# Moving the strip buffers and temporaries of an encoder kernel by 192 bytes within each SBUF partition

## The chip, the cores and the metric

The kernel runs on one core of one Trainium2 chip. The metric is the device time of one execution in microseconds; lower is better. Before the change it is 2692.87 us, the median of three runs (2691.46 to 2693.15).

## The reference

Two layers of a bidirectional encoder on 256 tokens with 2048 features, all in float32, and a final norm:

```python
for l in range(DEPTH):                                  # 2
    u = rmsnorm(x, norm_mix[l])
    proj = u @ w_in[l]                                  # 2048 x 8256
    c_q, c_kv, k_pe, q_na, k_na, v_na, gate_a, gate_b = jnp.split(proj, IN_SPLITS, axis=-1)
    q  = rmsnorm(c_q, norm_qa[l]) @ w_uq[l]             # latent attention, 8 heads
    kv = rmsnorm(c_kv, norm_kva[l]) @ w_ukv[l]
    ...
    y_a = mla_attention(q_nope, rope(q_pe), k_nope, rope(k_pe), v) @ w_o_mla[l]
    y_b = neighbourhood_attention(q_na, k_na, v_na, rpb[l]) @ w_o_na[l]
    merged = sigmoid(gate_a) * y_a + sigmoid(gate_b) * y_b
    x = x + merged @ w_out[l]                           # 2048 x 2048
    h = rmsnorm(x, norm_mlp[l]) @ w_ff1[l]              # 2048 x 8192
    x = x + jnp.square(relu(h)) @ w_ff2[l]              # 8192 x 2048
return rmsnorm(x, norm_final)
```

## The kernel before

**Precision.** Every large product is made of float32r matmuls on operands that are split in two: `hi`, the value cast to float32r, and `lo`, what the cast left out. A product is hi x hi + hi x lo + lo x hi, three matmuls of TensorE that add up in one PSUM bank.

**The two homes of the operands.** Activations live in *slots*: 46 tiles of 128 partitions x 512 float32, 2048 bytes a partition each, in the pool `slots` (`pair()`, `wide()`, lines 88 and 92). Weights come from HBM as *strips*: 1 MB lands in `raw` by a DMA from SyncE's queue, ScalarE casts it into `hi`, VectorE subtracts into `lo` (lines 194 and 195 in the attention half of a layer, 170 and 171 in the MLP half and the output projection). Three `raw` buffers let the loads run ahead. Strips live in the pools `wpool` and `wpool2`, temporaries in `tmp` and `tmp2`; the first of each pair is opened for the attention half of a layer and closed after it, the second for the other half, at the same addresses.

**Who streams and who is loaded.** A matmul of TensorE first loads a 128 x 128 piece of one operand into the array (the stationary operand, PEld in the profile) and then streams the other through it (the moving operand). Three helpers use the two homes differently:
- `mm_b` (lines 216 and 217) loads a piece of a strip and streams a slot: 512 wide with `hi`, which covers hi and lo of the activation at once, then 256 wide with `lo`. It makes the projections whose result is wanted transposed.
- `mm_a` (lines 225 to 227) and `mm3` in `gemm_s` (line 381) load a piece of a slot and stream 512 columns of a strip, three matmuls per product. They make the gates, the output projections and, in `gemm_s` with Strassen's scheme on some of the blocks, the MLP. In the latent attention's values `mm_a` streams 256 columns.
- `mm_3` (lines 230 to 232) serves attention: for the scores both operands are slots, for softmax times values the moving one is `pp`, a temporary.

**Order of the work.** The order is written out in the kernel's Python code, with small generators for the attention heads and transposes that are advanced between groups of matmuls (`tick`), and a scheduler that places the instructions. Nothing in it reads an address.

**Where things lie in a partition.** Pools are laid out one behind the other as they are opened: `const`, `slots`, `keep`, then the pools of weights and temporaries. `const` ends, and so the slots begin, on a multiple of 256 bytes. Within a pool the tiles are laid out in the order of their first use, each rounded up to 32 bytes. `keep` holds, in this order, two `sums`, `junk`, two `var`, six `rcol`, four `diag` and four `rrow`: 64 + 2048 + 64 + 192 + 2048 + 4096 bytes. The buffers of strips are multiples of 4096 bytes, so all of them begin at the same place within 256 bytes as the pool itself. The buffers of `tmp` follow the strips in the same partition.

Of the kernel before, what the change touches and what calls it, by code (L numbers as in the profile page):

```python
# [33 lines left out]
F32 = mybir.dt.float32  # L34
# [5 lines left out]
P = 128  # L40
# [31 lines left out]
def trunk(ctx: ExitStack, tc: tile.TileContext, x, w_in, w_uq, w_ukv, rpb, w_o_mla, w_o_na,  # L72
# [4 lines left out]
    keep = ctx.enter_context(tc.tile_pool(name="keep", bufs=2))  # L77
# [17 lines left out]
    def small():  # L95
        return tmp.tile([P, S], F32, tag="small", name="small", bufs=smalls)

    ident = const.tile([P, P], F32, name="ident")
    make_identity(nc, ident)
    ones = const.tile([P, P], F32, name="ones")  # L100
# [788 lines left out]
```

## Time and profile before

| | before |
|---|---|
| median of three runs | 2692.87 us |
| the profiled execution, its own time | 2693.53 us |
| its span, first to last instruction | 2691.8 us |
| mean granted TensorE clock | 0.996 |
| matmuls | 12606 |
| TensorE busy | 2653.6 us |
| weight loads (beside the matmuls) | 2208.0 us |
| VectorE busy | 1912.8 us |
| ScalarE busy | 1387.9 us |
| moved by DMA | 508.92 MB, 189 GB/s on average |

In the profile's groups of instructions a line names the source line, the engine (PE is the matmul, PEld the load of weights, DVE is VectorE, ACT ScalarE), the operation, the tile written and the tiles read, the shapes, the count, then the sum of busy time in us and the mean of one in ns, and last the engine's idle time before them with what ended it. `pair`, `vh`, `vl` and `wide` are slots; `hi`, `lo`, `raw` and, in `gemm_s`, `sums` are strips. The chain of waits follows the work that ended last back from the last instruction; its pieces have a start, a length and what they were.

### The profile page before, as it was taken

What the parts mean: (1) busy time and instruction counts of PE and PEld (TensorE: products, weight loads), DVE (VectorE), ACT (ScalarE), POOL (GpSimd) and SP (SyncE); (2) the same over time, 40 slices, a digit from 0 to 9 for tenths busy, and PEclk for the clock granted to TensorE, in tenths of its full rate; (3) what the DMA queues carried; (4) which work ended last, traced back from release to release, by engine and by line L of the source; (5) the groups of instructions that cost most, each with busy time, mean ns of one, the idle gap of its engine ahead of it and who ended that gap; (6) DMA issues with size and microseconds to landing.
All of it is one profiled execution on the core that took longest, in us unless ns stands there. A gap on an engine that the chain in (4) does not pass through costs nothing.

```text
span 2691.8 us, 31697 instructions
## 1 busy us (share of the span) xinstructions
PE 2653.6 (99%) x12606; PEld 2208.0 (82%) x12606; DVE 1912.8 (71%) x2172; ACT 1387.9 (52%) x1611; POOL 95.1 (4%) x122
## 2 busy tenths in 40 slices
PE   8999999999999999999999999999999999999998
PEld 7888888878888888888878888888788888888886
DVE  5675486556788887887666754855567888878885
ACT  5554464445555545546445544644455555455453
POOL 1100000000000010000001000000000000100000
PEclk9999999999999999999999999999999999999999
DMA  7555544554667585675555555455645665766754
GB/s 231 184 155 189 192 153 156 187 187 166 205 193 234 166 240 190 201 234 174 187 173 175 169 188 184 145 164 170 210 168 196 203 219 180 234 203 196 250 167 146
DMA packets 199300, 508.92 MB, mean 189 GB/s; under 512 B 13456, under 2 KB 17552, under 8 KB 199152
## 3 DMA queue, kind: packets, MB, share of 16 engines
q1 hardware_dynamic: 189184, 488.14, 55.5%
q0 software_dynamic: 8960, 17.14, 3.2%
q8 instruction: 98, 1.61, 0.2%
q10 hardware_dynamic: 1008, 1.61, 0.2%
q14 instruction: 50, 0.41, 0.0%
HBM read 492.18 MB, written 2.10 MB: 184 GB/s over the span
## 4 chain that ended last, share of the span: by engine, by line
PE 90%; issue 7%; DVE 1%; ACT 1%; DMA 1%; POOL 0%; POOLq 0%; DVEq 0%; ACTq 0%
PE bank L381 42%; PE bank L227 11%; PE bank L225 11%; PE bank L226 11%; PE bank L216 8%; PE bank L217 4%; PE bank L344 1%; PE bank L230 1%; PE bank L232 1%; PE bank L231 1%; DMA raw<-in_w_in 1%; ACT hi L170 0%; PE bank L494 0%; PE bank L443 0%; DVE lo L195 0%
## 5 line engine op out<-in xcount | busy, mean ns | idle before, releaser
L381 PE MATMUL bank<-hi,pair 128*128 128x512 f32 x3692 | 1154.9, 392 | 3.2 <-ACT hi L170 3.2
L381 PEld LDWEIGHTS bank<-hi,pair 128*128 128x128 f32 x3692 | 692.2, 188 | 160.0 <-ACT hi L170 10.0
L171 DVE TENSOR_TENSOR lo<-raw,hi 128x2048 fp32r<-128x2048 f32 (+1 forms) x288 | 618.3, 2150 | 190.4 <-ACT hi L170 189.2
L170 ACT CAST hi<-raw 128x2048 fp32r<-128x2048 f32 (+1 forms) x288 | 517.3, 1801 | 452.5 <-PE bank L381 299.3
L381 PE MATMUL bank<-lo,pair 128*128 128x512 f32 x1846 | 723.3, 392 | 0.0
L195 DVE TENSOR_TENSOR lo<-raw,hi 128x1024 fp32r<-128x1024 f32 (+1 forms) x352 | 426.3, 1214 | 351.5 <-ACT hi L194 349.5
L194 ACT CAST hi<-raw 128x1024 fp32r<-128x1024 f32 (+1 forms) x352 | 364.3, 1041 | 410.4 <-PE bank L227 295.5
L225 PE MATMUL bank<-hi,pair 128*128 128x512 f32 (+1 forms) x1344 | 522.4, 390 | 0.0
L227 PE MATMUL bank<-hi,pair 128*128 128x512 f32 (+1 forms) x1344 | 520.9, 388 | 0.0
L226 PE MATMUL bank<-lo,pair 128*128 128x512 f32 (+1 forms) x1344 | 517.5, 385 | 2.4 <-DVE lo L171 2.4
L381 PEld LDWEIGHTS bank<-lo,pair 128*128 128x128 f32 x1846 | 346.8, 188 | 75.5 <-DVE lo L171 1.4
L216 PE MATMUL bank<-pair,hi 128*128 128x512 f32 x960 | 347.5, 403 | 5.5 <-ACT hi L194 4.8
L226 PEld LDWEIGHTS bank<-lo,pair 128*128 128x128 f32 x1344 | 252.9, 188 | 54.8 <-DVE lo L171 2.9
L227 PEld LDWEIGHTS bank<-hi,pair 128*128 128x128 f32 x1344 | 252.8, 188 | 54.4
L225 PEld LDWEIGHTS bank<-hi,pair 128*128 128x128 f32 x1344 | 252.9, 188 | 48.6
L217 PE MATMUL bank<-pair,lo 128*128 128x256 f32 x960 | 268.0, 283 | 0.0
L171 DVE TENSOR_TENSOR lo<-sums,hi 128x2048 fp32r<-128x2048 f32 x74 | 169.6, 2292 | 112.9 <-ACT hi L170 112.9
L170 ACT CAST hi<-sums 128x2048 fp32r<-128x2048 f32 x74 | 141.4, 1911 | 184.0 <-DVE sums L409 153.2
L216 PEld LDWEIGHTS bank<-pair,hi 128*128 128x128 f32 x960 | 181.8, 190 | 45.1 <-ACT hi L194 5.2
L217 PEld LDWEIGHTS bank<-pair,lo 128*128 128x128 f32 x960 | 181.5, 190 | 1.8
L424 DVE TENSOR_TENSOR wide<-wide,bank 128x512 f32<-128x512 f32 x240 | 154.0, 679 | 0.3
L405 DVE TENSOR_TENSOR sums<-raw 128x1024 f32<-128x1024 f32 x74 | 90.2, 1219 | 14.4 <-DMA raw<-in_w_ff 14.1
(122 smaller groups left out, 1463.0 us busy)
## 6 DMA issues: line engine op xcount, KB each, us to landing
raw<-in_w_ff SPq DMA_DIRECT2D x256, 1024.0 KB, 5.3
raw<-in_w_in SPq DMA_DIRECT2D x124, 1024.0 KB, 5.2
raw<-in_w_out SPq DMA_DIRECT2D x32, 1024.0 KB, 5.2
raw<-in_w_o_na SPq DMA_DIRECT2D x16, 1024.0 KB, 5.2
raw<-in_w_o_mla SPq DMA_DIRECT2D x16, 1024.0 KB, 5.2
xt<-wide POOLq DMA_DIRECT2D x48, 256.0 KB, 7.2
raw<-in_w_ukv SPq DMA_DIRECT2D x8, 1024.0 KB, 5.1
raw<-in_w_uq SPq DMA_DIRECT2D x8, 768.0 KB, 4.6
```

Source lines behind the costliest of these rows:

```text
L170: nc.scalar.copy(hi, src)
L171: nc.vector.tensor_tensor(lo, src, hi.bitcast(F32), op=ALU.subtract)
L194: nc.scalar.copy(hi, src)
L195: nc.vector.tensor_tensor(lo, src, hi.bitcast(F32), op=ALU.subtract)
L216: nc.tensor.matmul(ps, wh, a, start=first, stop=False)
L217: nc.tensor.matmul(ps[:, :S], wl, a[:, :S], start=False, stop=last)
L225: nc.tensor.matmul(ps, ah, wh, start=first, stop=False)
L226: nc.tensor.matmul(ps, ah, wl, start=False, stop=False)
L227: nc.tensor.matmul(ps, al, wh, start=False, stop=last)
L381: nc.tensor.matmul(b[i], x, y, start=count[i] == 1, stop=count[i] == total[i])
L405: nc.vector.tensor_tensor(ts[:, :1024].rearrange("p (a n) -> p a n", a=2), raw[:, :512].rearrange("p (a n) -> p a n", a=1).to_broadcast([P ...
L424: add = lambda o, a, c: nc.vector.tensor_tensor(o, a, c, op=ALU.add)
```

## The change

One tile of 48 float32, 192 bytes a partition, is taken from the pool `keep` before anything else is. It is never written or read. `keep` grows by 192 bytes, its other tiles and all pools opened behind it move up by as much, and strips begin at a multiple of 256 bytes, as slots do. `const` and the slots stay where they are. The instructions of all engines, their order and their waits are those of before; source lines behind the new ones count two higher.

```diff
     def small():
         return tmp.tile([P, S], F32, tag="small", name="small", bufs=smalls)
 
+
+    keep.tile([P, 48], F32, name="phase", bufs=1)
     ident = const.tile([P, P], F32, name="ident")
     make_identity(nc, ident)
     ones = const.tile([P, P], F32, name="ones")
```

## The prediction

> Places are given below as the remainder of an operand's address within a partition, divided by 256 bytes; "64/0" means that the moving operand (the one streamed through the array) begins at place 64 and the stationary one (the weights loaded into it) at place 0. About 0.2% (5.4 us) is what a measurement of this kernel can tell from no change.
>
> **What bounds the kernel now.** First the page: busy times, granted clock, chain of waits.
>
> ```profile
> span 2691.8 us, 31697 instructions
> PE 2653.6 (99%) x12606; PEld 2208.0 (82%) x12606; DVE 1912.8 (71%) x2172; ACT 1387.9 (52%) x1611; POOL 95.1 (4%) x122
> ...
> PEclk9999999999999999999999999999999999999999
> ...
> PE 90%; issue 7%; DVE 1%; ACT 1%; DMA 1%; POOL 0%; POOLq 0%; DVEq 0%; ACTq 0%
> ```
>
> TensorE is busy from end to end at full granted clock, and 97% of the chain is PE or its "issue" gaps. Everything else has slack, also in the densest stage, the MLP (table by stretches, first column PE, then PEld, DVE, ACT):
>
> ```profile
> 1110.00:1210.00 100.00, 100.00 (x437) 81.74 (x436) 83.01 (x65) 47.20 (x29) 7.07 (x8) 1.00 0.74 226
> ```
>
> There DVE has 17 us of 100 to spare and the DMA engines a quarter. So the time is 12,606 matmuls times the distance from one start to the next (the pitch), and only a changed pitch moves it. Next, which matmuls there are, from the groups by shape (x is the count, then total us and mean ns; a duration contains the pipeline, so it is longer than the pitch):
>
> ```profile
> L381 PE MATMUL bank<-hi,pair 128*128 128x512 f32 x3692 | 1154.9, 392 | 3.2 <-ACT hi L170 3.2
> L381 PE MATMUL bank<-lo,pair 128*128 128x512 f32 x1846 | 723.3, 392 | 0.0
> L225 PE MATMUL bank<-hi,pair 128*128 128x512 f32 x1280 | 504.5, 395 | 0.0
> L227 PE MATMUL bank<-hi,pair 128*128 128x512 f32 x1280 | 503.0, 393 | 0.0
> L226 PE MATMUL bank<-lo,pair 128*128 128x512 f32 x1280 | 499.6, 390 | 2.4 <-DVE lo L171 2.4
> ...
> L216 PE MATMUL bank<-pair,hi 128*128 128x512 f32 x960 | 347.5, 403 | 5.5 <-ACT hi L194 4.8 <-DVE pair L164 0.8
> ...
> L217 PE MATMUL bank<-pair,lo 128*128 128x256 f32 x960 | 268.0, 283 | 0.0
> ...
> L231 PE MATMUL bank<-pair 128*128 128x256 f32 x96 | 27.5, 286 | 0.0
> L232 PE MATMUL bank<-pair 128*128 128x256 f32 x96 | 27.2, 284 | 0.0
> L230 PE MATMUL bank<-pair 128*128 128x256 f32 x96 | 27.1, 282 | 0.0
> ...
> L225 PE MATMUL bank<-hi,pair 128*128 128x256 f32 x64 | 17.9, 280 | 0.0
> L226 PE MATMUL bank<-lo,pair 128*128 128x256 f32 x64 | 17.9, 280 | 0.0
> L227 PE MATMUL bank<-hi,pair 128*128 128x256 f32 x64 | 17.9, 280 | 0.0
> ...
> L232 PE MATMUL bank<-pp,vl 128*128 128x256 f32 x32 | 9.0, 281 | 0.0
> ...
> L231 PE MATMUL bank<-pp,vh 128*128 128x256 f32 x32 | 9.0, 280 | 0.0
> ```
>
> Four kinds, by where their operands lie now. Strips streamed against slots (L381, L225 to L227): 64/0. Slots streamed against strips (L216, L217, a 512-wide and a 256-wide one in turn): 0/64. Slots against slots (L230 to L232 with "pair" alone, the attention scores): 0/0. Softmax tiles against slots ("pp"): 192/0. The same 256-wide matmul stands here in all four: 283 at 0/64, 280 at 64/0, 280 to 281 at 192/0, and 282 to 286, mean 284, at 0/0, the arrangement that the change gives to the first two kinds.
>
> Durations have modelled ends, so I read pitches from the chain of waits in order of time (start us, us, what), as first and last row of an unbroken run:
>
> ```profile
> 700.98 42.83 PE bank L381 x187
> ```
> ```profile
> 53.50 0.12 PE bank L217
> ...
> 63.75 0.12 PE bank L217
> ```
> ```profile
> 371.99 0.12 PE bank L230
> ...
> 373.43 0.23 PE bank L216
> ```
> ```profile
> 374.84 0.12 PE bank L225
> ...
> 377.67 0.23 PE bank L216
> ```
> ```profile
> 383.78 0.12 PE bank L230
> ...
> 384.48 0.22 PE bank L464
> ```
>
> In order: 512 wide at 64/0, 42.83 / 187 = 229.0 ns. The pair at 0/64: 29 pairs in 10.25 us, 353.4 ns a pair. 256 wide at 0/0: 12 in 1.44 us, 120.0 ns. 256 wide at 64/0: 24 in 2.83 us, 117.9 ns. 256 wide at 192/0: 6 in 0.70 us, 116.7 ns (rounding leaves about 1 ns, 0.4 ns and 2 ns on the last three; the mean durations rank them the same way).
>
> **The change, part by part.** The pool `keep` holds 64 + 2048 + 64 + 192 + 2048 + 4096 = 8512 bytes a partition (small tiles take 32), which is 33 x 256 + 64, and it follows the slots, which lie on multiples of 256. That is why strips begin at 64. 192 more make them begin at 0; the addresses in the built program say the same, so the change does what it says. No instruction is added, removed or moved on any engine, no wait is added, and nothing writes the reserved bytes. What can change is how long instructions take.
>
> *Strips as moving operand, 64/0 to 0/0.* 5538 (L381) + 3840 (L225 to L227) = 9378 of 512 wide and 192 of 256 wide. No row shows a 512-wide one at 0/0, so it is bounded. The nearest rows are the two 256-wide runs: 120.0 - 117.9 = +2.1 ns at 0/0. Both kinds load 128 x 128 weights while the matmul before streams:
>
> ```profile
> L381 PEld LDWEIGHTS bank<-hi,pair 128*128 128x128 f32 x3692 | 692.2, 188 | 160.0 <-ACT hi L170 10.0
> ...
> L232 PEld LDWEIGHTS bank<-pair 128*128 128x128 f32 x96 | 18.2, 189 | 0.0
> ```
>
> That is one load per matmul and no longer for the wider one, so I take +2.1 ns per matmul whatever its width: 9570 x 2.1 = +20.1 us. If instead it goes with the streamed columns, 120.0 / 117.9 is +1.8%, +4.1 ns on 229.0: 9378 x 4.1 + 192 x 2.1 = +38.9 us. The other bound lies below nothing and is worked out under the faster rival. One row speaks on the 512-wide case directly, a slots-moving matmul (0) ahead of weights at 0 (TensorE in order of time):
>
> ```profile
> 102.74 0.39 PE L216 MATMUL bank<-pair,hi 128*128 128x512 f32 x1
> 102.97 0.28 PE L230 MATMUL bank<-pp,vh 128*128 128x256 f32 x1
> ```
>
> 0.23 us: between 229 and 231 cannot be told at this rounding, but it is not the 235 of its neighbours (353.4 - 118).
>
> *Strips as weights, 0/64 to 0/0.* 960 pairs at 353.4 ns. By the first value a pair becomes (229.0 + 2.1) + 120.0 = 351.1: 960 x -2.3 = -2.2 us. By the second it is 233.1 + 120.0 = 353.1: -0.3 us.
>
> *The rest.* `pp` goes from 192 to 128: 96 matmuls between 116.7 and 120.0, at most +0.3 us; the transposes of the softmax (128) and the small float32 matmuls shift by less than that each. DVE and ACT read and write strips at the new place too:
>
> ```profile
> L408 DVE TENSOR_TENSOR sums<-raw,sums 128x512 f32<-128x512 f32 x74 | 50.6, 684 | 0.5
> ...
> L800 DVE TENSOR_TENSOR xt<-xt,wide 128x512 f32<-128x512 f32 x8 | 5.1, 680 | 0.0
> ```
>
> The first has all three operands at 64, the second all at 0: 4 ns, on an engine with slack. Zero for the end. Weights land 5 us after their issue, three buffers ahead; only the load at the start, which nothing covers, could move, by tenths of a us.
>
> Sum against the profiled execution's own 2693.5 us: +20.1 - 2.2 = +17.9, 2711.4. The median of the runs is 0.7 below that execution, so the forecast is 2710.8, rounded to 2711. By the columns: +38.6, 2731.
>
> **A rule against the row.** The 0/0 run takes 120.0 ns and the 64/0 run 117.9. The Trainium skill, SBUF — State Buffer, section "SBUF: two separate sides", says that among the engines only the port pair shared by VectorE and GpSimd makes anyone wait, and that TensorE never does; by that the time would stay at 2693. The 2.1 ns speak against it as far as one kind of matmul can.
>
> **The rivals.**
>
> *Nothing changes (same).* The 2.1 ns at 0/0 could belong to the attention scores and not to the place: they come in short runs of 6 or 12 between other matmuls. For: the four kinds lie within 3% of each other at 256 wide. Against: the softmax-times-values matmuls run in the same helper, in runs as short, and are not slower than 64/0. Time: 2693, give or take 5.
>
> *The same place is the best place (faster).* The mechanism is that the cost falls with the distance between the two starts. For: at 0/64 (192 round the 256) a 512-wide matmul takes 353.4 - 118 = 235 ns against 229 at 64/0, so arrangement matters and 64 apart beats 192 apart; 0 could be better again. If the step to 0 is half of that step of 6.4, 3.2 ns: 9378 x -3.2 = -30.0 us, and the pairs fall to 225.8 + 117.9 = 343.7, 960 x -9.7 = -9.3 us; together -39, 2654. It decides as soon as the 512-wide pitch falls below 229.0 - 5.4 / 9378 x 1000 = 228.4 ns; a small gain of 1 ns gives 2681. Against: the only 0/0 run there is. DVE, with 17% spare in the MLP, would not take over for a gain of 1.5%.
>
> The pitch at 64/0 is 229.0 ns. The Trainium skill, TensorE: Matmul & The Clock Gate, "Part 2: What happens when you issue a matmul", gives about 216 ns from one 512-wide matmul to the next; if the place were all that keeps this kernel from it, the time would be 9378 x 13 = 122 us lower, 2571 (an estimate from that page). No run here shows 216.
>
> *By the columns (slower still).* 2731, as worked out above. For: the 512-wide durations differ more between kinds (392 to 403) than the 256-wide (280 to 286).
>
> **How the numbers follow.** Slower 0.52: per matmul 0.36, by the columns 0.16. Same 0.22. Faster 0.26, because 0/0 at 512 wide was never seen, and of the two kinds seen at 512 the one with strips as weights at 64 is the slow one. The likeliest case's own range is 2700 to 2732. For 8 in 10 I take that case nearly whole (0.50), same whole (0.22) and the small gains (0.11): from 2665 to 2732.
>
> **What would show it.** In the profile after, the order of instructions and the counts are those of before, and PE stays near 99%. Right: the long L381 runs of the chain at 231 ns instead of 229.0, with mean durations up from 392; the pair near 351; the 0/0 scores still at 120.0. By the columns: 233. Same: 229.0 and 353.4. The faster rival: below 228.4. Wrong altogether would be a change of time with an unchanged pitch, which would then lie in idle time of PE, now under 2%.

## The result and the profile after

The change makes the kernel faster: 2675.34 us (2673.55 to 2676.27, six runs) against 2692.16 us before (six runs), a ratio of 0.9936 with a 95% interval of 0.9924 to 0.9949. That is 16.8 us, where 18 us the other way had been forecast.

The page of the profiled execution after (2675.85 us; source lines count two higher than before):

```profile
span 2674.1 us, 31697 instructions
...
PE 2636.0 (99%) x12606; PEld 2206.9 (83%) x12606; DVE 1912.9 (72%) x2172; ACT 1388.7 (52%) x1611; POOL 95.4 (4%) x122
...
PEclk9999999999999999999999999999999999999999
...
PE 85%; issue 7%; DVE 5%; ACT 2%; DMA 1%; POOL 0%; POOLq 0%; DVEq 0%; ACTq 0%
```

The counts are the same, the clock is the same, VectorE and ScalarE are as busy as before to 0.1%. TensorE alone is busy for 17.6 us less, and the span is 17.7 us shorter: the whole effect is TensorE's. In the chain 5% of the span have passed from TensorE to the casts of DVE and ACT: strips are now ready only just in time at places. That costs little so far: the idle time before the Strassen matmuls (first row below) went from 3.2 to 4.3 us, and TensorE's idle time as a whole, span less busy time, stayed at 38 us.

The groups by shape after, in the order of those shown of before:

```profile
L383 PE MATMUL bank<-hi,pair 128*128 128x512 f32 x3692 | 1147.3, 390 | 4.3 <-ACT hi L172 3.3
L383 PE MATMUL bank<-lo,pair 128*128 128x512 f32 x1846 | 720.0, 390 | 0.0
...
L227 PE MATMUL bank<-hi,pair 128*128 128x512 f32 x1280 | 500.8, 392 | 0.0
L228 PE MATMUL bank<-lo,pair 128*128 128x512 f32 x1280 | 500.5, 391 | 2.4 <-DVE lo L173 2.4
L229 PE MATMUL bank<-hi,pair 128*128 128x512 f32 x1280 | 500.0, 391 | 0.0
...
L218 PE MATMUL bank<-pair,hi 128*128 128x512 f32 x960 | 346.3, 403 | 4.2 <-ACT hi L196 3.8 <-DVE pair L166 0.4
L219 PE MATMUL bank<-pair,lo 128*128 128x256 f32 x960 | 266.9, 282 | 0.0
...
L233 PE MATMUL bank<-pair 128*128 128x256 f32 x96 | 27.5, 286 | 0.0
...
L229 PE MATMUL bank<-hi,pair 128*128 128x256 f32 x64 | 18.1, 283 | 0.0
L228 PE MATMUL bank<-lo,pair 128*128 128x256 f32 x64 | 18.1, 283 | 0.0
```

The same lines of code move in opposite directions. 512 wide, L383 goes from 392 to 390, and L227 and L229 from 395 and 393 to 392 and 391. L228, the middle one of the three in `mm_a`, gains nothing at 512 wide: 390 before, 391 after. 256 wide, L228 and L229 go from 280 to 283. The pair that loads strips (L218, L219) and the attention scores (L233) stay within 1 ns.

The pitches from the chain after, each as an unbroken run or its first and last piece: the Strassen matmuls, the pair, the scores, the values.

```profile
696.15 42.43 PE bank L383 x187
```
```profile
53.13 0.12 PE bank L219
...
63.02 0.12 PE bank L219
```
```profile
369.23 0.12 PE bank L232
...
370.67 0.24 PE bank L218
```
```profile
372.09 0.12 PE bank L227
...
374.96 0.23 PE bank L218
```

42.43 / 187 = 226.9 ns, where it was 229.0. The pair: 28 in 9.89 us, 353.2 (353.4). The scores: 12 in 1.44 us, 120.0 (120.0). The values, 256 wide, now 0/0: 24 in 2.87 us, 119.6 (117.9). Worked out from these runs: 9378 x -2.1 = -19.7 us, 192 x +1.7 = +0.3, 960 x -0.2 = -0.2; together -19.6, beside -17.7 of the span. The same matmuls stand in the same order in both traces, so the distances from start to start can be added up by line over the whole of both. The Strassen matmuls come to -9.4 us, waits included; L227, L228 and L229 at 512 wide to -3.8, +0.8 and -2.6; the pairs to -1.7; the values to +0.3; all others to -1.4. Together that is the span's -17.7, up to rounding. So 2.1 ns for each of the 9378 is too much. The Strassen sum holds the 1.1 us of idle time named above, and the middle matmul of `mm_a` ran at 227.1 ns already before (mean from start to start, waits left out; 227.2 after), while the other two went from 230.4 and 229.6 to 227.1.

### The profile page after: what moved, and what is told of

It is laid out like the page before. It is cut to its first block, busy times and chain, and to the rows that moved or that the text cites. A ratio compares the mean times of both kernels' runs of the same rounds, so it can differ in the third digit from the quotient of the medians.

```text
span 2674.1 us, 31697 instructions
## 1 busy us (share of the span) xinstructions
PE 2636.0 (99%) x12606; PEld 2206.9 (83%) x12606; DVE 1912.9 (72%) x2172; ACT 1388.7 (52%) x1611; POOL 95.4 (4%) x122
## 4 chain that ended last, share of the span: by engine, by line
PE 85%; issue 7%; DVE 5%; ACT 2%; DMA 1%; POOL 0%; POOLq 0%; DVEq 0%; ACTq 0%
PE bank L383 36%; PE bank L228 11%; PE bank L229 11%; PE bank L227 11%; PE bank L218 8%; PE bank L219 4%; DVE lo L173 2%; ACT hi L172 2%; PE bank L346 1%; PE bank L232 1%; PE bank L234 1%; PE bank L233 1%; DVE pair L361 1%; PE bank L496 0%; DMA raw<-in_w_in 0%
## 5 line engine op out<-in xcount | busy, mean ns | idle before, releaser
L383 PE MATMUL bank<-hi,pair 128*128 128x512 f32 x3692 | 1147.3, 390 | 4.3 <-ACT hi L172 3.3
L383 PEld LDWEIGHTS bank<-hi,pair 128*128 128x128 f32 x3692 | 691.8, 188 | 153.7 <-ACT hi L172 11.0
L383 PE MATMUL bank<-lo,pair 128*128 128x512 f32 x1846 | 720.0, 390 | 0.0
L228 PE MATMUL bank<-lo,pair 128*128 128x512 f32 (+1 forms) x1344 | 518.5, 386 | 2.4 <-DVE lo L173 2.4
L227 PE MATMUL bank<-hi,pair 128*128 128x512 f32 (+1 forms) x1344 | 518.9, 387 | 0.0
L229 PE MATMUL bank<-hi,pair 128*128 128x512 f32 (+1 forms) x1344 | 518.1, 386 | 0.0
L383 PEld LDWEIGHTS bank<-lo,pair 128*128 128x128 f32 x1846 | 346.6, 188 | 72.8 <-DVE lo L173 1.8
L218 PE MATMUL bank<-pair,hi 128*128 128x512 f32 x960 | 346.3, 403 | 4.2 <-ACT hi L196 3.8
L228 PEld LDWEIGHTS bank<-lo,pair 128*128 128x128 f32 x1344 | 253.4, 189 | 51.5 <-DVE lo L173 2.9
L229 PEld LDWEIGHTS bank<-hi,pair 128*128 128x128 f32 x1344 | 253.4, 189 | 50.7
L227 PEld LDWEIGHTS bank<-hi,pair 128*128 128x128 f32 x1344 | 253.1, 188 | 49.1
L219 PE MATMUL bank<-pair,lo 128*128 128x256 f32 x960 | 266.9, 282 | 0.0
L218 PEld LDWEIGHTS bank<-pair,hi 128*128 128x128 f32 x960 | 181.2, 189 | 43.6 <-ACT hi L196 4.2
L219 PEld LDWEIGHTS bank<-pair,lo 128*128 128x128 f32 x960 | 181.9, 190 | 1.7
L407 DVE TENSOR_TENSOR sums<-raw 128x1024 f32<-128x1024 f32 x74 | 90.2, 1219 | 11.7 <-DMA raw<-in_w_ff 11.4
```

The costliest lines, as they stand in the source:

```text
L218: nc.tensor.matmul(ps, wh, a, start=first, stop=False)
L219: nc.tensor.matmul(ps[:, :S], wl, a[:, :S], start=False, stop=last)
L227: nc.tensor.matmul(ps, ah, wh, start=first, stop=False)
L228: nc.tensor.matmul(ps, ah, wl, start=False, stop=False)
L229: nc.tensor.matmul(ps, al, wh, start=False, stop=last)
L383: nc.tensor.matmul(b[i], x, y, start=count[i] == 1, stop=count[i] == total[i])
```

## The experiments

Three theories at the start. **A**: what counts is the distance between the starts of the streamed and the loaded operand within 256 bytes, and at 512 columns distance 0 is best. **B**: the streamed strip's own place counts, a multiple of 256 being best. **C**: the operands don't matter, the shifted temporaries do. In A, which operand is loaded when the matmul streams is left open. No kernel leaves work out. Pitches below are from the same run of 187 Strassen matmuls in the chain, unless said otherwise. In the code cuts, the remarks behind `#` are added here; they stand in no kernel.

### The distance: 128, 192, 32 and 224 bytes

The tile in `keep` takes another size.

```diff
-    keep.tile([P, 48], F32, name="phase", bufs=1)
+    keep.tile([P, 16], F32, name="phase", bufs=1)   # strips at 128; 32: 192; 56: 32; 40: 224
```

> Strips at place 128, slots at 0 (64 bytes reserved instead of 192). Theory A, the distance between the starts of the streamed and the loaded operand counts and 0 is best: the 512-wide strip matmul is at or above the 229.0 ns of 64 apart, the time 2692 us or more. Theory B, only the streamed strip's own place counts and a multiple of 256 is best: as with 64, 229 ns and 2692 us. Theory C, operands do not matter and the shift of the temporaries did it: between 2675 and 2693 us with the pitch of whatever the temporaries' place gives. The 256-wide matmul: A and B both have no number for it.

> Strips at place 192, slots at 0 (128 bytes reserved). Theory A: at or above 229.0 ns at 512 wide, 2692 us or more; if the distance counts round the 256 bytes, 192 is like 64 and gives 229.0 ns. Theory B: 229 ns, 2692 us. The 256-wide softmax matmuls that streamed from 192 before took 116.7 ns against 117.9 at 64, so 256 wide 116 to 118 ns here.

> 224 bytes reserved: strips at 32, slots at 0. If the pitch goes smoothly with the distance: halfway between 0 (227.1) and 64 (229.0), 228 ns, 2684 us. If there is a single best place and any distance costs the same or more: 229 ns or above, 2692 us or more. If the best place lies between 0 and 64: under 227 ns, under 2674 us.

> 160 bytes reserved: strips at 224, 32 bytes short of the slots' place. Smoothly between 192 (233.4 ns) and 0 (227.1): 230 ns, 2703 us. If any start behind the slots' place costs in full: 233 ns, 2730 us. If the best place lies here: under 227 ns, under 2674 us.

Measured: 2725.09 us at 128 (ratio to before 1.0120, 1.0105 to 1.0135), 2730.26 at 192 (1.0142, 1.0126 to 1.0159), 2728.21 at 32 (1.0133, 1.0118 to 1.0148), 2726.44 at 224 (1.0123, 1.0108 to 1.0138). The runs in the chain, in the order 128, 192, 32, 224:

```profile
706.77 43.62 PE bank L382 x187
```
```profile
706.88 43.63 PE bank L382 x187
```
```profile
708.58 43.63 PE bank L382 x187
```
```profile
707.42 43.62 PE bank L382 x187
```

All four are 233.3 ns. So of six distances, 0 gives 226.9, 64 gives 229.0 and the four others the same 233.3 in this run, though their times lie up to 5 us apart. B is out in the form put forward, since all places but 0 should have been alike and 64 is not. So is a cost that grows with the distance: 32 is dearer than 64. So is a best place between: nothing tried is under 226.9. The kernel before stood at the second best of the six places. At 256 columns the order is another one: the latent attention's values take, from start to start, 119.6 ns on average at distance 0, 118.7 at 128, 118.2 at 224, 117.9 at 64, 117.0 at 32 and 116.9 at 192 (180 starts each).

### Whose place: the slots moved, or both

```diff
     xt = [const.tile([P, D], F32, name=f"xt{t}") for t in range(2)]
+    const.tile([P, 48], F32, name="phase_slots")    # slots at 192, strips at 0
```

and, for both at 64, 16 float32 there and the 48 of the change in `keep`.

> 192 bytes are reserved ahead of the slots instead: slots at 192, strips at 0, which is 64 apart as before, but the strips lie where the change puts them. Theory A: pitch 229.0 ns at 512 wide and 2692 us, as before. Theory B: 226.7 ns and 2675 us, as after the change.

> Slots and strips both begin at 64 (64 bytes ahead of the slots, 192 more in the pool behind them). Theory A: starts are equal, so 226.7 ns at 512 wide and 2675 us, as after the change. Theory B: the strips are off the multiple of 256, so 229.0 ns and 2692 us.

Measured: 2691.89 us (0.9997, 0.9988 to 1.0006) with the slots at 192 and the strips at 0; 2674.19 us (0.9933, 0.9918 to 0.9947) with both at 64.

```profile
698.05 42.82 PE bank L382 x187
```
```profile
694.99 42.45 PE bank L383 x187
```

229.0 and 227.0 ns. The strips stand at 0 in the first and don't gain; they stand at 64 in the second, as before the change, and gain all of it. For the Strassen matmuls A is borne out and B excluded: it is the distance, wherever the two lie.

### Is it 256 bytes, and is it the temporaries

448 bytes in `keep` instead of 192; and 192 bytes at the head of `tmp` and `tmp2` alone.

```diff
-    keep.tile([P, 48], F32, name="phase", bufs=1)
+    keep.tile([P, 112], F32, name="phase", bufs=1)
```
```diff
         tmp = half_a.enter_context(tc.tile_pool(name="tmp", bufs=2, reuse_waits="tile"))
+        tmp.tile([P, 48], F32, name="phase", bufs=1)   # likewise in tmp2; nothing in keep
```

> 448 bytes are reserved, 256 more than in the change: strips at 0 within 256 bytes, 256 further within 512 or more. Theory A (the distance within 256 bytes decides): 227.1 ns at 512 wide and 2675 us, as after the change. Rival (a longer period, 512 bytes or more, decides): another pitch, anywhere from 227 to 233 ns, 2675 to 2730 us.

> 192 bytes are reserved ahead of the temporaries alone: strips stay at 64, temporaries move to where the change puts them. Theories A and B: 229.0 ns at 512 wide, 2692 us, as before. Theory C, the shift of the temporaries (transposes, softmax tiles, evacuations) did it: 2675 us.

Measured: 2676.73 us (0.9938, 0.9923 to 0.9953) and 2692.33 us (0.9998, 0.9989 to 1.0008).

```profile
695.05 42.43 PE bank L382 x187
```
```profile
700.48 42.83 PE bank L381 x187
```

256 bytes more change nothing: 226.9 ns. That 256 is the period, and not a longer one up to 2048 bytes, can be seen within two other traces as well, with the addresses of the built program set beside the matmuls. Before, the Strassen matmuls stand at four distances within 2048 bytes (320, 832, 1344 and 1856, all 64 within 256), and the mean from start to start is 228.9 to 229.1 ns at each. In the kernel with slots 2304 bytes apart, used further below, they stand at all eight multiples of 256, and it is 227.0 to 227.4 ns at each. The temporaries alone leave 229.0: C is out.

### Which half of the layer

```diff
         wpool = half_b.enter_context(tc.tile_pool(name="wpool2", bufs=4, reuse_waits="tile"))
+        wpool.tile([P, 48], F32, name="phase", bufs=1)  # nothing in keep
```

> 192 bytes are reserved ahead of the strips of the second half of each layer alone (output projection and MLP): 5538 matmuls of the Strassen products and 960 of the plain ones stream from 0, the other 2880 stay at 64, and the pairs that load strips stay as before. Theories A and B: 6498 of 9378 matmuls gain 2.3 ns at the most, 15 us, so 2677 to 2681 us; and the rest of the gain lies in the attention half. Were the loaded strips of the attention half the seat of the gain: 2690 us or more.

Measured: 2681.31 us (0.9958, 0.9942 to 0.9975), 11.4 us less than before, beside 16.8 for the whole change.

```profile
698.64 42.43 PE bank L381 x187
```

The moved half runs at 226.9 ns; 6498 x 2.1 = 13.6 us, and 11.4 are measured. So 6498 of the 9378 matmuls, 69%, carry 68% of the gain. The gain goes roughly by the number of matmuls that stream strips at 512 wide, but not evenly among the three of `mm_a`, as shown above; 2.1 ns for each is again too much.

### Width: the Strassen matmuls in halves

The step of the prediction that failed is tested directly: the matmuls of `gemm_s` are cut into two of 256 columns, with the strips at 64 and at 0.

```diff
-                nc.tensor.matmul(b[i], x, y, start=count[i] == 1, stop=count[i] == total[i])
+                if count[i] in (1, total[i]):
+                    nc.tensor.matmul(b[i], x, y, start=count[i] == 1, stop=count[i] == total[i])
+                    continue
+                for h in (0, 256):
+                    nc.tensor.matmul(b[i][:, h:h + 256], x, y[:, h:h + 256], start=False, stop=False)
```

> Strips at 64 as before, but in the Strassen products all matmuls save the first and last of a bank are cut into two of 256 columns: 5058 of 512 wide become 10116 of 256 wide. By the pitches of before (117.9 and 229.0 ns) 5058 x 6.8 ns are added: 2727 us. It is the base for the next run.

> The same cut with the strips at 0. If what a place costs depends on the width (0 is better for 512 columns and worse for 256, 119.9 against 117.9 ns): the 10116 narrow matmuls lose 20 us and the 4320 left at 512 wide gain 9, so about 11 us slower than the run with the strips at 64, 2738 us: the change's sign is turned round. If the place is better at any width (fewer 256-byte blocks touched, say): 17 us or more faster than that run.

Measured: 2719.71 us with strips at 64 and 2738.05 at 0. The same 192 bytes make this kernel 18.3 us slower. Runs of the chain with strips at 64, then at 0:

```profile
679.09 9.66 PE bank L385 x82
...
1149.86 18.47 PE bank L385 x163
```
```profile
677.24 9.83 PE bank L386 x82
...
1156.68 19.55 PE bank L386 x163
```

At 64: 117.8 ns, and 113.3 in the longest runs. At 0: 119.9 ns in both. Cutting the matmuls turns the sign of the place round, in the same loop, on the same engine and data. The 113.3 ns were not expected; they explain most of the 7 us by which the first kernel is under its forecast, and of the difference of 18 instead of 11 us: with the strips at 64, 1344 of the narrow matmuls start 112 to 115 ns apart, where most others average 117.9, together 6 us.

The cut changes more than the width of a matmul: it doubles the weight loads per column, and each piece of weights is loaded twice in a row. What it does not change are the first and last matmul of each bank, 480 of 512 columns, which now stand among narrow ones. The groups at 64 and at 0, the narrow ones first:

```profile
L385 PE MATMUL bank<-hi,pair 128*128 128x256 f32 x6424 | 1053.9, 280 | 2.2 <-ACT hi L170 2.2
...
L382 PE MATMUL bank<-hi,pair 128*128 128x512 f32 x480 | 182.7, 394 | 0.0
```
```profile
L386 PE MATMUL bank<-hi,pair 128*128 128x256 f32 x6424 | 1071.6, 284 | 1.7 <-ACT hi L171 1.7
...
L383 PE MATMUL bank<-hi,pair 128*128 128x512 f32 x480 | 183.7, 396 | 0.0
```

These 480 are 512 wide and at distance 0 in the second kernel, yet they lose as the narrow ones do: 394 to 396 ns, and 231.5 to 234.0 from start to start. So the sign does not hang on a matmul's own width alone; 512 columns gain at distance 0 in a stream of their like.

### Which weights: those in the array or those being loaded

While a matmul streams, the next one's weights are loaded, so the distance could be to either. First all slots are laid 2112 bytes apart, so that they lie at 0, 64, 128 and 192 in turn, with the strips at 0.

```diff
-        return slots.tile([P, 512], F32R, tag="slot", name="pair")
+        return slots.tile([P, 528], F32R, tag="slot", name="pair")[:, :512]   # wide, vh, vl alike
...
+    keep.tile([P, 16], F32, name="phase", bufs=1)
```

> Slots are 2112 bytes apart instead of 2048, so they lie at 0, 64, 128 and 192 in turn; strips at 0. Over all matmuls the distances are about even: mean pitch 230.6 ns (of 227.1, 229.0, 233.0, 233.4), 2708 us. Its use is in the split of the pitch by the slot in the array (own weights) and by the slot that is loaded meanwhile (the next matmul's weights): theory A1, the load that runs beside the streaming decides: the pitch follows the distance to the next weights and not to the own. Theory A2, the weights in the array decide: the other way round.

Measured: 2709.76 us (1.0062, 1.0045 to 1.0078), where the mean over the four distances had given 2708.

```profile
702.45 43.24 PE bank L382 x187
```

231.2 ns in this run, between the levels. The mean of the levels is thus a fair forecast of this mixture. But with the addresses of the built program set beside the trace, the means from start to start are 230.3, 232.4, 231.9 and 231.7 ns for own weights 0, 64, 128 and 192 away, and 231.5, 230.4, 231.8 and 231.9 for the next weights: neither follows the levels 227, 229 and 233, and the question stayed open. So the lo slots of the Strassen products alone were moved, by 32 and by 128 bytes, in slots of 2304 bytes, of which 44 fit, with four small temporaries instead of eight.

```diff
-NSLOT, SMALL, RBUFS, HBUFS = 46, 8, 3, 4
+NSLOT, SMALL, RBUFS, HBUFS = 44, 4, 3, 4
...
+        return slots.tile([P, 576], F32R, tag="slot", name="pair")[:, off:off + 512]
...
-            h, lw = pair(), pair()
+            h, lw = pair(), pair(8)      # base: pair(0); at 128: pair(32)
```

> Base for the next two: slots 2304 bytes apart, 44 instead of 46, four small temporaries instead of eight, strips at 0, everything at 0. Pitch of the Strassen products 227.1 ns at each of the three matmuls of a product; the time may differ from 2675 us by the fewer buffers.

> As the base, but the slots with the lo halves that the Strassen products load begin at 32; hi slots and strips stay at 0. The three matmuls of a product are hi x hi (own weights 0 away, next 0), hi x lo (own 0, next 32 away), lo x hi (own 32 away, next 0). Theory A1, the load beside the streaming decides: the second of the three goes from 227.1 to 233.3 ns, the third stays. Theory A2, the weights in the array decide: the third goes to 233.3 ns, the second stays. Either way 1846 x 6.2 ns = 11 us more than the base. If both count, 2 x 11 us.

> As the run with the lo slots at 32, but at 128. A1: the second of the three at 232.8 ns; A2: the third. About 10 us over the base.

Measured: 2703.02 us for the base, 28 above the change. Of the 26.6 us by which its span is longer, 17.6 are idle time of TensorE (55.7 us beside 38.1); that the fewer buffers cause it was not tried apart. Then 2729.33 at 32 and 2722.09 at 128: 26 and 19 us over the base, nearer to twice 11 than to once. TensorE in order of time; a row "lo" is the second matmul of a product, the "x2" behind it its third and the first of the next. Base, 32, 128:

```profile
697.38 0.39 PE L382 MATMUL bank<-lo,pair 128*128 128x512 f32 x1
...
700.10 0.39 PE L382 MATMUL bank<-lo,pair 128*128 128x512 f32 x1
```
```profile
697.53 0.40 PE L382 MATMUL bank<-lo,pair 128*128 128x512 f32 x1
697.77 0.62 PE L382 MATMUL bank<-hi,pair 128*128 128x512 f32 x2
...
699.63 0.40 PE L382 MATMUL bank<-lo,pair 128*128 128x512 f32 x1
```
```profile
697.22 0.39 PE L382 MATMUL bank<-lo,pair 128*128 128x512 f32 x1
697.45 0.62 PE L382 MATMUL bank<-hi,pair 128*128 128x512 f32 x2
...
700.00 0.40 PE L382 MATMUL bank<-lo,pair 128*128 128x512 f32 x1
```

Base: four products in 2.72 us, 680 ns each. At 32: three in 2.10 us, 700 ns, 20 more, of which the second matmul takes 0.24 us. At 128: four in 2.78 us, 695 ns, 15 more, with 0.23 us for the second. Over all Strassen matmuls of the traces the mean pitches of first, second and third are 227 each in the base; 231, 235 and 232 ns at 32; 227, 232 and 234 ns at 128. By A1 only the second would move, by A2 only the third. Both do at 128, all three at 32. One displaced operand of three costs as much at 32 as if all were displaced (3 x 233.3 = 700), and three quarters of it at 128. So neither theory holds alone. That the first matmul moves at 32, with its own and the next weights both at distance 0, fits neither, nor the two together; how the cost arises stays open.

## Why the prediction was wrong

**What bounds the kernel** was right: the order and all counts stayed, and the span moved by TensorE's busy time to 0.1 us. So was the part on the change itself: only the time of matmuls moved.

**That the place moves the pitch** was right, and so was the 256-wide price where only 256-wide matmuls follow each other: the values went from 117.9 to 119.6 ns where 120.0 was said, and the scores stayed at 120.0.

**The step that failed** is "so I take +2.1 ns per matmul whatever its width", the term of +20.1 us. It carried a difference measured at 256 columns to 9378 matmuls of 512. In the streams of 512-wide matmuls that fill the kernel they went the other way, 229.0 to 226.9: about the size, by chance, with the other sign. From start to start the 9378 came to -15.0 us where +20 had been put. The halves show the step in one loop: cut to 256 columns, the matmuls lose at 0 about what they gain uncut. They don't show that the width of a matmul alone decides, since the 480 left at 512 columns among narrow ones lost 2.4 ns; why the sign turns stays open. The bound by the columns was wrong by the same step. The one row at 512 wide, 0.23 us, was a poor guide: 18 such matmuls stand in the trace, 230 to 232 ns each from start to start, but their own weights lay at 64 and they stood among pairs. No row of before had a 512-wide matmul with the own weights 0 apart, so the sign was not there to be read. With that, 0.52 against 0.26 was too sure. The range, 2665 to 2732, holds 2675 only because it took in the small gains of a rival; the case that the forecast stood on does not.

**The pair** was put at 351.1 and is 353.2 in the run shown. Over the whole trace the 960 pairs come to -1.7 us where -2.2 had been put, and that is luck. The forecast had the 512-wide matmul fall from 235 to 231 ns and the 256-wide one rise from 118 to 120. Over 786 unbroken pairs the means from start to start went from 234.2 to 235.0 and from 118.4 to 116.6, each the other way. The 480 of the halves, 512 columns among 256, did not gain either, so the mixture is a likely reason; no run changes the mixture alone. Nor does the distance settle the pair: with both operands at 64, again 0 apart, the same stretch of the chain runs faster, 31 pairs in 10.75 us, 346.8 ns each.

```profile
53.01 0.11 PE bank L219
...
63.76 0.12 PE bank L219
```

**The rival that came true**, "the same place is the best place", had the sign, half again the size (3.2 ns for 2.1) and the wrong mechanism: by it the cost falls with the distance, and 32 bytes cost 233.3 ns where 64 cost 229.0. Its -9.3 us on the pairs did not come. Its time, 2654, lay below the result.

**The rule weighed against the row.** Six distances moved the pitch between 226.9 and 233.3 ns with the instructions unchanged. The Trainium skill, SBUF — State Buffer, section "SBUF: two separate sides", has TensorE wait for nobody among the engines. No run here shows it waiting for another engine's access, so that sentence is not refuted; what the runs refute is the step from it to "the time would stay at 2693", because the pitch moved with the distance between TensorE's own two operands. The best pitch seen at 512 columns is 226.9 ns. The Trainium skill, TensorE: Matmul & The Clock Gate, "Part 2: What happens when you issue a matmul", gives a gap of about 216 ns; it was not reached at any place.

## What to carry to other kernels

Where TensorE is busy from end to end, read its pitch from unbroken runs of the chain, and try where streamed and loaded operands begin relative to each other: here 2675 to 2730 us lay between places, at the price of one unused tile. Don't carry a pitch from one width to another, not even its sign; measure the width that fills the kernel, in the stream in which it stands. In a kernel like this one, an edit that shifts a pool by a small tile can gain or lose as much as this by the shift alone, so compare such edits at the same place.

## What the runs showed of the hardware

The pitch does not go smoothly with the place. At 512 columns six distances gave three values, 226.9, 229.0 and 233.3 ns, four of them the same one; at 256 columns 113.3, 117.8 and 119.9 appeared in the halves, the first two with the same addresses modulo 256. In streams of one width, the distance that is best at 512 columns (0: 226.9 ns) is the worst at 256 (values, 119.6 ns); among matmuls of the other width, 512 columns at distance 0 took 234 to 235. No version beat the change: both operands at 64 (2674.19 us) and 256 bytes further (2676.73) agree with it within the runs' spread.
